# Final RMSNorm of a decoder step on one core: the mean by wide F32 products, the root on ScalarE, the last block in token halves

## The chip, the core and the metric

The kernel runs on one core of one Trainium2 chip. The core has TensorE (PE, matrix products into PSUM), VectorE (DVE), ScalarE (ACT), GpSimd (POOL) and SyncE (SP, which here only issues DMAs). The metric is the time of one execution in microseconds on the device; lower is better. Three runs of the kernel before lasted 1084.12, 1084.95 and 1085.59 us, so the median is 1084.95 us.

## The reference

One layer of a decoder trunk on 256 prompt tokens and 8 x 4 sample tokens with 2048 channels, all in F32, and a final norm over the channels. What matters here is the end:

```python
def rmsnorm(x, g):
    xf = x.astype(jnp.float32)
    y = xf * lax.rsqrt(jnp.mean(xf * xf, axis=-1, keepdims=True) + EPS)
    return (y * g.astype(jnp.float32)).astype(x.dtype)
...
    h2 = rmsnorm(x, norm2_g)
    f = jnp.square(jax.nn.relu(jnp.einsum("btd,df->btf", h2, w_ff1)))
    x = x + jnp.einsum("btf,fd->btd", f, w_ff2)
...
    y_prompt = rmsnorm(xp, norm_f)
    y_sample = rmsnorm(xs, norm_f)
```

Before that stand an input projection, a depthwise convolution with a layernorm, a pooling group and an output projection.

## The kernel before

Activations lie with channels on the partitions: `xT` is 128 x 16 x 288, sixteen blocks k of 128 channels by T = 288 tokens. All weights stream once from HBM in pieces of 128 x 1024 F32. ScalarE rounds each piece to F32R (`whi`, L274), VectorE or GpSimd forms the rest (`wlo`, L279, L282), and `gemm` makes three products for each 128 x 128 weight tile (L305), each with 288 moving columns. The feed-forward part runs in four chunks of 2048 hidden channels: eight groups of the first product, then eight groups g of the second, each group two output blocks k = 2g and 2g + 1.

The order of the instructions on each engine is set by a scheduler that plays the program through; `tc.issue_after(...)` ties a piece of code to stand behind a given instruction.

The second norm (`second_rows`, L638 to L651) comes once, inside the first chunk: a mean by two products with the constant tile `means`, a `Sqrt` on ScalarE (L648), and `inverse_root` (L231 to L236): a reciprocal and one Newton step in three SCALAR_TENSOR_TENSOR operations on VectorE, all 128 x 288 wide.

In the last chunk (`last`, L682 to L692) each block of `xT` gets its product added (L683), ScalarE squares it (L686, L689), VectorE adds the square into `ssf` (L691), and ScalarE multiplies the block by the gain of the final norm (L692). For the last block, k = 15, the square stays in `qf`.

The end of the kernel, from L698:

- L703: the sums over the channels. For each of three runs of 96 tokens, the 96 columns of `ssf`, then of `qf`, are the stationary side and one column of the constant `mean_d` is the moving side. The means stand as 96 x 3 in PSUM (`ends`).
- L706: products `idle<-ones`, three behind the `ssf` sums and four behind the `qf` sums, whose result is not used.
- L708 and `inverse_root`: square root, reciprocal and Newton step on 96 x 3.
- L712: the row spread. Products with the identity put the inverse root of each token on all 128 partitions, once in PSUM as `rows_f` (in `ends`) and once more as `again`.
- `finish` (L716 to L721): VectorE multiplies the blocks 0 to 11 by `rows_f`, read from PSUM, in pieces of 1, 1, 2, 2, 3 and 3 blocks. L724: ScalarE copies `again` to `rf` in SBUF, and GpSimd, which here reads SBUF alone, multiplies the blocks 12 to 15 by `rf`, one by one. Each piece is stored as soon as it is done; the pieces of each engine go in turn to the queue of SP and the queue of ScalarE. One block of the output is 128 x 288 F32, 144 KB; all sixteen are 2304 KB.

Of the kernel before, what the change touches and what calls it, by code (L numbers as in the profile page):

```python
# [9 lines left out]
F32 = mybir.dt.float32  # L10
F32R = mybir.dt.float32r
AF = mybir.ActivationFunctionType
ALU = mybir.AluOpType
# [3 lines left out]
P = 128  # L17
# [3 lines left out]
T = SEQ + NB * NS  # L21
TB = T // 3
# [6 lines left out]
EPS = 1e-6  # L29
KT = D // P  # L30
# [7 lines left out]
ZO = PH + SEQ  # L38
ZL = ZO + NB * ZS
LATER = 1000000  # L40

# [43 lines left out]
def trunk_kernel(ctx: ExitStack, tc: tile.TileContext, io):  # L87
# [3 lines left out]
    nc = tc.nc  # L91

    const = ctx.enter_context(tc.tile_pool(name="const", bufs=1))
# [7 lines left out]
    cvp = ctx.enter_context(tc.tile_pool(name="cvp", bufs=2, space=PSUM))  # L101
# [4 lines left out]
    def nm(s):  # L106
        seen[s] = seen.get(s, 0) + 1
        return f"{s}{seen[s]}"

    @contextmanager  # L110
    def later(by=LATER):

        tc.cur_priority += by
        yield
        tc.cur_priority -= by

    def row(name):
        return rowp.tile([P, T], F32, name=nm(name), tag="row")
# [9 lines left out]
    def tmp(name, n=T, tag="tmp", bufs=2):  # L128
        return tmpp.tile([P, n], F32, name=nm(name), tag=tag, bufs=bufs)

    def ms(name):
        return msp.tile([P, 2, 512], F32, name=nm(name), tag="ms")

    def f32(t):
        return t.bitcast(F32)

    def both(r):

        return r[:, None, :T].to_broadcast([P, 2, T])
# [11 lines left out]
    xT = const.tile([P, KT, T], F32, name="xT")  # L151
# [4 lines left out]
    def v(key, j):  # L156
        return vec[:, OFF[key] + j : OFF[key] + j + 1]
# [45 lines left out]
    ones = const.tile([P, P], F32, name="ones")  # L203
# [3 lines left out]
    def load_table(func, src):  # L207

        return nc.scalar.activation(few[: src.shape[0], :], src, func)
# [5 lines left out]
    ident = const.tile([TB, TB], F32, name="ident", padded_shape=[TB, TB + 40])  # L215
# [7 lines left out]

    means = const.tile([P, P], F32R, name="means")
    nc.vector.tensor_scalar(means, ones, DC / D, None, op0=ALU.mult)
    cst = const.tile([P, 32], F32, name="cst")
    eps, mean_d = cst[:, 0:1], cst[:, 1:2]
    nc.vector.memset(eps, EPS)
    nc.vector.memset(mean_d, 1.0 / D)

    def inverse_root(mean, root, y, out):  # L231

        nc.vector.reciprocal(y, root)
        nc.vector.scalar_tensor_tensor(out=root, in0=mean, scalar=EPS, in1=y, op0=ALU.add, op1=ALU.mult)
        nc.vector.scalar_tensor_tensor(out=root, in0=root, scalar=-0.5, in1=y, op0=ALU.mult, op1=ALU.mult)
        nc.vector.scalar_tensor_tensor(out=out, in0=root, scalar=1.5, in1=y, op0=ALU.add, op1=ALU.mult)  # L236

    def rsqrt_sums(parts, scale, after=None):

# [62 lines left out]
    def mm(*args, **kw):  # L302

        with tc.issue_after(chain[-1]) if chain else nullcontext():
            last = nc.tensor.matmul(*args, **kw)  # L305
        if chain:
            chain[0] = last.ins
        return last
# [37 lines left out]
    def bank2():  # L346
        return acc.tile([P, 2, 512], F32, name=nm("ac"), tag="ac")

    def each(bk):
        return [bk[:, m, :] for m in range(2)]  # L350

    def halves(x2):

        return [(x2[0][:, m, :], x2[1][:, m, :]) for m in range(2)]
# [193 lines left out]
    load_table(AF.Sqrt, f32(mixp[1][0])[:, 0:1])  # L548
    with later(2 * LATER):
        nc.sync.dma_start(io["u_out"], u_all[:, :, UO - CH : UL])  # L550
# [30 lines left out]
    for g in range(8):  # L581
        bk = bank2()
        with behind:
            last = gemm(each(bk), [mixp[k] for k in korder], between=BETWEEN.get(g, {}), classes=TURN if g == 2 else "")
# [5 lines left out]
    for j, c in enumerate(cs):  # L590
        n = tmpp.tile([P, 2, T], F32, name=nm("n"), tag="ag", bufs=2)
# [12 lines left out]
    last = None  # L604
    for g in range(8):
        bk = bank2()
        last = gemm(each(bk), mixc, classes=TURN if g == 2 else "")
# [14 lines left out]
        for m, (ah, al) in enumerate(a2):  # L622
            k = 2 * g + m
            xk = xT[:, k, :]
# [13 lines left out]
    def second_rows():  # L638

        hl = actp.tile([P, 4, T], F32R, name="hl", tag="act")  # L640
        hi, lo = hl[:, 1, :], hl[:, 0, :]
        nc.scalar.copy(hi, ss2)
        nc.vector.tensor_tensor(lo, ss2, f32(hi), op=ALU.subtract)
        bk, r2 = ms("mean2"), row("r2")
        mean, root = bk[:, 0, :T], bk[:, 1, :T]
        mm(mean, means, hi, start=True, stop=False)
        last = mm(mean, means, lo, start=False, stop=True)
        nc.scalar.activation(root, mean, AF.Sqrt, bias=eps)  # L648
        inverse_root(mean, root, r2, r2)
        rows2.append(r2)  # L650
        return last  # L651

    for ch in range(DFF // FCH):
        fx, done = [], []
        for g in range(FCH // 256):
            bk = bank2()
            gemm(each(bk), x1, between={2: second_rows} if ch == 0 and g == 1 else {}, classes="01" * 6 + TURN if ch == 0 and g == 1 else "")
            if ch == 0 and g == 2:
                chain.clear()
            done.append(bk)  # L660
            if ch or g:
                for bk in done:
                    t = tmpp.tile([P, 2, T], F32, name=nm("t"), tag="ag", bufs=2)
                    nc.vector.scalar_tensor_tensor(out=t, in0=bk[:, :, :T], scalar=0.0, in1=both(rows2[0]), op0=ALU.max, op1=ALU.mult)  # L664
                    f = tmpp.tile([P, 2, T], F32, name=nm("f"), tag="ag2", bufs=2)
                    nc.scalar.activation(f, t, AF.Square)
                    fh, fl = act2("fx")
                    nc.scalar.copy(fh, f)
                    nc.vector.tensor_tensor(fl, f, f32(fh), op=ALU.subtract)
                    fx += halves((fh, fl))  # L670
                done = []
        last = ch == DFF // FCH - 1
        for g in range(8):
            bk = bank2()
            banks = each(bk)
            if last and g == 7:
                banks[1] = bank2()[:, 1, :]
            gemm(banks, fx, m_outer=last and g == 7)
            for m in range(2):
                k = 2 * g + m  # L680
                xk = xT[:, k, :]
                if last:  # L682
                    nc.vector.tensor_tensor(xk, xk, banks[m][:, :T], op=ALU.add)  # L683
                    if k == 0:
                        ssf = row("ssf")
                        nc.scalar.activation(ssf, xk, AF.Square)  # L686
                    else:
                        qf = tmp("q")
                        nc.scalar.activation(qf, xk, AF.Square)  # L689
                        if k < KT - 1:  # L690
                            nc.vector.tensor_tensor(ssf, ssf, qf, op=ALU.add)  # L691
                    nc.scalar.activation(xk, xk, AF.Copy, scale=v("norm_f", k))  # L692
                elif m:
                    x2 = xT[:, 2 * g : 2 * g + 2, :]
                    nc.vector.tensor_tensor(x2, x2, bk[:, :, :T], op=ALU.add)  # L695


    ends, again = ms("ends"), cvp.tile([P, 512], F32, name="again", tag="cv")[:, :T]  # L698
    sums_f, rows_f = ends[:TB, 0, 0:3], ends[:, 1, :T]
    idle = cvp.tile([P, 512], F32, name="idle", tag="cv")  # L700
    for n, (part, busy) in enumerate(((ssf, 3), (qf, 4))):
        for j in range(3):
            last = nc.tensor.matmul(sums_f[:, j : j + 1], part[:, j * TB : (j + 1) * TB], mean_d[:, 0:1], start=n + j == 0, stop=n == 1 and j == 2)  # L703
        with tc.issue_after(last.ins):
            for j in range(busy):
                nc.tensor.matmul(idle[:, 0:P], ones, ones, start=True, stop=True)  # L706
    root, first, s_f = [cst[:TB, 2 + 3 * j : 5 + 3 * j] for j in range(3)]
    nc.scalar.activation(root, sums_f, AF.Sqrt, bias=eps[:TB, :])  # L708
    inverse_root(sums_f, root, first, s_f)
    for spread_f in (rows_f, again):  # L710
        for j in range(3):
            nc.tensor.matmul(spread_f[:, j * TB : (j + 1) * TB], s_f[:, j : j + 1].to_broadcast([TB, P]), ident, start=j == 0, stop=j == 2)  # L712
    rf = row("rf")
    queues = (nc.sync, nc.scalar)

    def finish(eng, r, pieces):  # L716

        for j, (k0, n) in enumerate(pieces):
            xk = xT[:, k0 : k0 + n, :]
            eng.tensor_tensor(xk, xk, r[:, None, :].to_broadcast([P, n, T]), op=ALU.mult)  # L720
            queues[j % 2].dma_start(io["yT"][:, k0 : k0 + n, :], xk)  # L721

    finish(nc.vector, rows_f, ((0, 1), (1, 1), (2, 2), (4, 2), (6, 3), (9, 3)))
    nc.scalar.copy(rf, again)  # L724
    finish(nc.gpsimd, rf, [(k, 1) for k in range(12, KT)])


# [56 lines left out]
```

## Time and profile before

| what | value |
|---|---|
| median of three runs | 1084.95 us (1084.12 to 1085.59) |
| profiled execution, span from its first to its last instruction | 1082.8 us |
| mean granted TensorE clock over the span | 0.997 |
| busy: PE, DVE, ACT, POOL | 1071.5, 635.4, 479.0, 173.6 us |
| HBM read, written | 185.16 MB, 4.28 MB |
| TensorE's last product of the last `gemm` ends | 1069.54 us |
| last VectorE and GpSimd multiplication ends | 1077.5 and 1077.6 us |

The page has no time of the profiled execution but its span, which is 2.15 us below the median of the runs. "Span" counts from the first to the last instruction on any engine, the closing waits of SP among them. A row of the timeline has the start, the length, the engine, the line, the operation, what it writes and reads, the shape, and how often it stands there in a row; where it says x6, the length runs from the start of the first to the end of the last. A row of the groups has the busy time of all and the mean of one in ns. Idle time is shown with what ended it.

### The profile page before, as it was taken

How to read it: one execution, taken by the hardware profiler on the slowest of the kernel's cores; microseconds unless marked ns; L12 is line 12 of the kernel's file. 1: busy time of each engine (PE TensorE's matmuls, PEld its weight loads, DVE VectorE, ACT ScalarE, POOL GpSimd, SP SyncE). 2: the span in 40 equal slices, each digit the busy share in tenths (PEclk: the TensorE clock that was granted, in tenths of full speed). 3: DMA queues.
4: the chain of work that ended last, by engine and by line, in shares of the span. 5: the costliest groups of instructions: out<-in, count | busy, mean ns of one | idle time of the engine just before them, and what ended most of it. 6: DMA issues, size and time to landing. Idle time of an engine off the chain costs nothing.

```text
span 1082.8 us, 19572 instructions
## 1 busy us (share of the span) xinstructions
PE 1071.5 (99%) x8198; PEld 1069.9 (99%) x8198; DVE 635.4 (59%) x818; ACT 479.0 (44%) x585; POOL 173.6 (16%) x180
## 2 busy tenths in 40 slices
PE   9999999999999999999999999999999999999996
PEld 9999999999999999999999999999999999999996
DVE  8899999678655544445544444545544445554553
ACT  8654445475544433334443333444433334444441
POOL 0878979512000000000000000000000000000001
PEclk9999999999999999999999999999999999999998
DMA  9896468545555555555555555555555555555522
GB/s 325 281 273 185 137 196 239 176 152 177 173 164 170 172 166 169 174 164 169 171 168 168 175 165 169 174 167 167 174 165 168 174 169 165 173 166 168 173 78 88
DMA packets 58296, 190.71 MB, mean 176 GB/s; under 512 B 6240, under 2 KB 11232, under 8 KB 58208
## 3 DMA queue, kind: packets, MB, share of 16 engines
q1 hardware_dynamic: 56336, 184.35, 53.9%
q0 software_dynamic: 1008, 3.67, 1.9%
q8 instruction: 64, 1.05, 0.4%
q10 hardware_dynamic: 864, 1.44, 0.4%
q14 instruction: 24, 0.20, 0.1%
HBM read 185.16 MB, written 4.28 MB: 175 GB/s over the span
## 4 chain that ended last, share of the span: by engine, by line
PE 77%; issue 20%; ACT 1%; DVE 0%; DMA 0%; POOL 0%; POOLq 0%
PE ac L305 77%; PE pp L305 1%; DMA wr<-in_w 0%; ACT whi L274 0%; POOL xT L720 0%; ACT n L595 0%; DVE wlo L279 0%; PE pt L305 0%; PE pmean L305 0%; POOLq L770 0%; DVE xT L695 0%; DVE n L592 0%; ACT whi L364 0%; ACT mx L597 0%; DVE hx L367 0%
## 5 line engine op out<-in xcount | busy, mean ns | idle before, releaser
L274 ACT CAST whi<-wr 128x1024 fp32r<-128x1024 f32 (+1 forms) x332 | 348.0, 1049 | 551.4 <-PE ac L305 533.5
L279 DVE TENSOR_TENSOR wlo<-wr,whi 128x1024 fp32r<-128x1024 f32 x288 | 353.1, 1226 | 348.5 <-ACT whi L274 348.5
L305 PE MATMUL ac<-ax,whi 128*128 128x288 f32 x2048 | 351.0, 292 | 0.0
L305 PE MATMUL ac<-fx,whi 128*128 128x288 f32 x2048 | 350.2, 292 | 0.0
L305 PEld LDWEIGHTS ac<-ax,whi 128*128 128x128 f32 x2048 | 296.0, 187 | 0.0
L305 PEld LDWEIGHTS ac<-fx,whi 128*128 128x128 f32 x2048 | 295.6, 187 | 0.0
L305 PE MATMUL ac<-ax,wlo 128*128 128x288 f32 x1024 | 217.4, 292 | 0.0
L305 PE MATMUL ac<-fx,wlo 128*128 128x288 f32 x1024 | 216.4, 292 | 0.0
L305 PEld LDWEIGHTS ac<-ax,wlo 128*128 128x128 f32 x1024 | 162.6, 187 | 0.0
L305 PEld LDWEIGHTS ac<-fx,wlo 128*128 128x128 f32 x1024 | 162.3, 187 | 0.0
L305 PE MATMUL ac<-hx,whi 128*128 128x288 f32 x768 | 131.8, 295 | 1.2 <-DVE hx L367 1.2
L720 POOL TENSOR_TENSOR xT<-xT,rf 128x288 f32<-128x288 f32 x4 | 3.1, 795 | 800.1 <-ACT rf L724 800.1
L305 PEld LDWEIGHTS ac<-hx,whi 128*128 128x128 f32 x768 | 112.1, 190 | 1.4 <-ACT hx L369 1.4
L282 POOL TENSOR_TENSOR wlo<-wr,whi 128x512 fp32r<-128x512 f32 x74 | 100.3, 1410 | 35.3 <-ACT whi L274 34.3
L461 DVE SCALAR_TENSOR_TENSOR pc<-u_all,vec,pc 128x256 f32<-128x256 f32 x232 | 99.5, 483 | 1.9 <-ACT pc L458 0.7
L305 PE MATMUL ac<-hx,wlo 128*128 128x288 f32 x384 | 80.1, 294 | 0.0
L305 PEld LDWEIGHTS ac<-hx,wlo 128*128 128x128 f32 x384 | 61.1, 190 | 0.0
L305 PE MATMUL ac<-dx,whi 128*128 128x288 f32 x256 | 46.0, 296 | 0.0
L305 PE MATMUL ac<-mx,whi 128*128 128x288 f32 x256 | 45.1, 294 | 0.1
L664 DVE SCALAR_TENSOR_TENSOR t<-ac,r 128x576 f32<-128x576 f32 x32 | 24.2, 758 | 25.1 <-PE ac L305 25.1
L305 PEld LDWEIGHTS ac<-dx,whi 128*128 128x128 f32 x256 | 38.0, 188 | 0.2
L305 PEld LDWEIGHTS ac<-mx,whi 128*128 128x128 f32 x256 | 37.5, 188 | 0.6 <-ACT mx L597 0.4
(133 smaller groups left out, 533.6 us busy)
## 6 DMA issues: line engine op xcount, KB each, us to landing
wr<-in_w SPq DMA_DIRECT2D x335, 512.0 KB, 3.8
wlo<-in_w POOLq DMA_DIRECT2D x7, 512.0 KB, 7.7
xT<-in_xT SPq DMA_DIRECT2D x8, 288.0 KB, 7.3
wr<-in_w SPq DMA_DIRECT2D x5, 256.0 KB, 3.6
out_u_out<-u_all SPq DMA_DIRECT2D x1, 1208.0 KB, 9.3
u_all<-in_hist_c SPq DMA_DIRECT2D x8, 136.0 KB, 6.2
out_z_out<-z_all SPq DMA_DIRECT2D x1, 668.0 KB, 9.9
z_all<-in_hist_p SPq DMA_DIRECT2D x4, 152.0 KB, 7.5
```

Of the source, the lines that this page charges most:

```text
L274: nc.scalar.copy(hi, raw)
L279: nc.vector.tensor_tensor(lo, raw, f32(hi), op=ALU.subtract)
L282: nc.gpsimd.tensor_tensor(lo[:, j : j + 2, :], raw[:, j : j + 2, :], f32(hi[:, j : j + 2, :]), op=ALU.subtract)
L305: last = nc.tensor.matmul(*args, **kw)
L461: nc.vector.scalar_tensor_tensor(out=dst, in0=up[:, w : w + SEQ], scalar=cwv[:, w : w + 1], in1=pc, op0=ALU.mult, op1=ALU.add)
L664: nc.vector.scalar_tensor_tensor(out=t, in0=bk[:, :, :T], scalar=0.0, in1=both(rows2[0]), op0=ALU.max, op1=ALU.mult)
L720: eng.tensor_tensor(xk, xk, r[:, None, :].to_broadcast([P, n, T]), op=ALU.mult)
```

## The change

Five things, all in the norms:

- `mean_d` becomes a constant tile of 128 x 128. The mean of the final norm is made by products in which `mean_d` is the stationary side and 144 token columns of `ssf` or `qf` the moving side, so that each mean stands on all 128 partitions at once. The products of L703, the unused products of L706 and the row spread of L712 go, and the copy of L724 with them.
- `inverse_root` takes ScalarE's `Abs_reciprocal_sqrt` for the first value in place of `Sqrt` and VectorE's reciprocal; three SCALAR_TENSOR_TENSOR operations stay. Both norms use it. In the final norm it now works on 128 x 144 twice, from PSUM into `rf` in SBUF.
- The last block, k = 15, is added and squared in two token halves, and the root is made for each half. Its gain is multiplied in behind the second root.
- VectorE and GpSimd both multiply by `rf` in SBUF.
- VectorE's pieces are now 1, 1, 1, 1, 2, 3 and 3 blocks.

```diff
+HALVES = (slice(0, T // 2), slice(T // 2, T))
...
-    cst = const.tile([P, 32], F32, name="cst")
-    eps, mean_d = cst[:, 0:1], cst[:, 1:2]
+    eps = const.tile([P, 32], F32, name="cst")[:, 0:1]
     nc.vector.memset(eps, EPS)
+    mean_d = const.tile([P, P], F32, name="mean_d")
     nc.vector.memset(mean_d, 1.0 / D)
-    def inverse_root(mean, root, y, out):
-        nc.vector.reciprocal(y, root)
-        nc.vector.scalar_tensor_tensor(out=root, in0=mean, scalar=EPS, in1=y, op0=ALU.add, op1=ALU.mult)
-        nc.vector.scalar_tensor_tensor(out=root, in0=root, scalar=-0.5, in1=y, op0=ALU.mult, op1=ALU.mult)
-        nc.vector.scalar_tensor_tensor(out=out, in0=root, scalar=1.5, in1=y, op0=ALU.add, op1=ALU.mult)
+    def inverse_root(mean, half, y):
+        root = nc.scalar.activation(y, mean, AF.Abs_reciprocal_sqrt, bias=eps)
+        nc.vector.scalar_tensor_tensor(out=half, in0=y, scalar=-0.5, in1=y, op0=ALU.mult, op1=ALU.mult)
+        nc.vector.scalar_tensor_tensor(out=half, in0=mean, scalar=EPS, in1=half, op0=ALU.add, op1=ALU.mult)
+        nc.vector.scalar_tensor_tensor(out=y, in0=half, scalar=1.5, in1=y, op0=ALU.add, op1=ALU.mult)
+        return root
...
-        nc.scalar.activation(root, mean, AF.Sqrt, bias=eps)
-        inverse_root(mean, root, r2, r2)
+        inverse_root(mean, tmp("q"), r2)
...
+                if last and k == KT - 1:
+                    qf = tmp("q")
+                    for h in HALVES:
+                        nc.vector.tensor_tensor(xk[:, h], xk[:, h], banks[m][:, h], op=ALU.add)
+                    for h in HALVES:
+                        nc.scalar.activation(qf[:, h], xk[:, h], AF.Square)
...
+    ends, rf, step = ms("ends"), row("rf"), tmp("q")
+    for n, h in enumerate(HALVES):
+        total = ends[:, n, h]
+        for part in (ssf, qf):
+            nc.tensor.matmul(total, mean_d, part[:, h], start=part is ssf, stop=part is qf)
+    for n, h in enumerate(HALVES):
+        root = inverse_root(ends[:, n, h], step[:, h], rf[:, h])
+    with tc.issue_after(root.ins):
+        nc.scalar.activation(xT[:, KT - 1, :], xT[:, KT - 1, :], AF.Copy, scale=v("norm_f", KT - 1))
...
-            eng.tensor_tensor(xk, xk, r[:, None, :].to_broadcast([P, n, T]), op=ALU.mult)
+            eng.tensor_tensor(xk, xk, rf[:, None, :].to_broadcast([P, n, T]), op=ALU.mult)
...
-    finish(nc.vector, rows_f, ((0, 1), (1, 1), (2, 2), (4, 2), (6, 3), (9, 3)))
-    nc.scalar.copy(rf, again)
-    finish(nc.gpsimd, rf, [(k, 1) for k in range(12, KT)])
+    finish(nc.vector, ((0, 1), (1, 1), (2, 1), (3, 1), (4, 2), (6, 3), (9, 3)))
+    finish(nc.gpsimd, [(k, 1) for k in range(12, KT)])
```

The scheduler leaves the order of all engines as it was up to the second norm and again from there to the last block, but for a few neighbours behind the second norm that change places. The end is another program. VectorE before, from the last block on (in brackets the engines that an instruction waits for):

```order
L683 TENSOR_TENSOR xT<-xT,ac_11386 128x288 [waits PE_49]
L233 RECIPROCAL cst<-cst 96x3 [waits Activation_49]
L234 SCALAR_TENSOR_TENSOR cst<-ends_11492,cst 96x3 [waits DVE_49,PE_49]
L235 SCALAR_TENSOR_TENSOR cst<-cst 96x3 [waits DVE_49]
L236 SCALAR_TENSOR_TENSOR cst<-cst 96x3 [waits DVE_49]
L720 TENSOR_TENSOR xT<-xT,ends_11492 128x288 [waits PE_49]
L720 TENSOR_TENSOR xT<-xT,ends_11492 128x288
L720 TENSOR_TENSOR xT<-xT,ends_11492 128x576 x2
L720 TENSOR_TENSOR xT<-xT,ends_11492 128x864 x2
```

VectorE now, at the same place (`q_11496` is `step`; the line numbers are the new ones):

```order
L686 TENSOR_TENSOR xT<-xT,ac_11387 128x144 [waits PE_49]
L686 TENSOR_TENSOR xT<-xT,ac_11387 128x144
L235 SCALAR_TENSOR_TENSOR q_11496<-rf_11495 128x144 [waits DVE_49,Activation_49]
L236 SCALAR_TENSOR_TENSOR q_11496<-ends_11494,q_11496 128x144 [waits DVE_49,PE_49]
L237 SCALAR_TENSOR_TENSOR rf_11495<-q_11496,rf_11495 128x144 [waits DVE_49]
L235 SCALAR_TENSOR_TENSOR q_11496<-rf_11495 128x144 [waits Activation_49]
L236 SCALAR_TENSOR_TENSOR q_11496<-ends_11494,q_11496 128x144 [waits DVE_49]
L237 SCALAR_TENSOR_TENSOR rf_11495<-q_11496,rf_11495 128x144 [waits DVE_49]
L719 TENSOR_TENSOR xT<-xT,rf_11495 128x288 [waits DVE_49]
L719 TENSOR_TENSOR xT<-xT,rf_11495 128x288 x3
L719 TENSOR_TENSOR xT<-xT,rf_11495 128x576
L719 TENSOR_TENSOR xT<-xT,rf_11495 128x864 x2
```

Six operations on 128 x 144 stand where four on 96 x 3 stood, and the multiplications read `rf` where they read `ends`. ScalarE with its queue before, from the last block's square on:

```order
L689 ACTIVATE q_11489<-xT 128x288 [waits DVE_49]
L692 ACTIVATE xT<-xT,vec 128x288 [waits Activation_49]
L708 ACTIVATE cst<-ends_11492,cst 96x3 [waits PE_49]
L724 COPY rf_11519<-again 128x288 [waits PE_49]
L721 DMA out_yT<-xT 128x288 [waits DVE_49]
L721 DMA out_yT<-xT 128x576 [waits DVE_49]
L721 DMA out_yT<-xT 128x288 [waits Pool_49]
L721 DMA out_yT<-xT 128x864 [waits DMAHW5_49,DVE_49]
L721 DMA out_yT<-xT 128x288 [waits DMAHW6_49,Activation_49,Pool_49]
```

And now:

```order
L688 ACTIVATE q_11489<-xT 128x144 [waits DVE_49] x2
L234 ACTIVATE rf_11495<-ends_11494,cst 128x144 [waits PE_49]
L234 ACTIVATE rf_11495<-ends_11494,cst 128x144 [waits DVE_49]
L712 ACTIVATE xT<-xT,vec 128x288 [waits Activation_49]
L720 DMA out_yT<-xT 128x288 [waits DVE_49]
L720 DMA out_yT<-xT 128x288 [waits Pool_49]
L720 DMA out_yT<-xT 128x288 [waits DVE_49]
L720 DMA out_yT<-xT 128x864 [waits DVE_49]
L720 DMA out_yT<-xT 128x288 [waits DMAHW6_49,Pool_49]
```

The gain of block 15 moved behind the second root, and the second root waits for VectorE: in the built program for its L236 of the first half, which reads the same PSUM tile. The first root waits for the last of the four products, so for both halves. In ScalarE's queue the stores are those of the blocks 1, 13, 3, 6 to 8 and 15, in this order; in SP's queue those of 0, 12, 2, 4 to 5, 14 and 9 to 11.

More of the change, by code (lines that the diff above doesn't have):

```diff
@@ L644, in second_rows @@
         bk, r2 = ms("mean2"), row("r2")
-        mean, root = bk[:, 0, :T], bk[:, 1, :T]
+        mean = bk[:, 0, :T]
         mm(mean, means, hi, start=True, stop=False)
         last = mm(mean, means, lo, start=False, stop=True)
-        nc.scalar.activation(root, mean, AF.Sqrt, bias=eps)
-        inverse_root(mean, root, r2, r2)
+        inverse_root(mean, tmp("q"), r2)
         rows2.append(r2)
@@ L681, in trunk_kernel @@
                 xk = xT[:, k, :]
-                if last:
+                if last and k == KT - 1:
[4 more added lines that the diff above has]
+                        nc.scalar.activation(qf[:, h], xk[:, h], AF.Square)
+                elif last:
                     nc.vector.tensor_tensor(xk, xk, banks[m][:, :T], op=ALU.add)
@@ L689, in trunk_kernel @@
                         nc.scalar.activation(qf, xk, AF.Square)
-                        if k < KT - 1:
-                            nc.vector.tensor_tensor(ssf, ssf, qf, op=ALU.add)
+                        nc.vector.tensor_tensor(ssf, ssf, qf, op=ALU.add)
                     nc.scalar.activation(xk, xk, AF.Copy, scale=v("norm_f", k))
@@ L695, in trunk_kernel, with finish @@
                     nc.vector.tensor_tensor(x2, x2, bk[:, :, :T], op=ALU.add)
[L698 to L713, printed above, removed]
+    ends, rf, step = ms("ends"), row("rf"), tmp("q")
[7 more added lines that the diff above has]
+        nc.scalar.activation(xT[:, KT - 1, :], xT[:, KT - 1, :], AF.Copy, scale=v("norm_f", KT - 1))
     queues = (nc.sync, nc.scalar)
-    def finish(eng, r, pieces):
+    def finish(eng, pieces):
         for j, (k0, n) in enumerate(pieces):
             xk = xT[:, k0 : k0 + n, :]
-            eng.tensor_tensor(xk, xk, r[:, None, :].to_broadcast([P, n, T]), op=ALU.mult)
+            eng.tensor_tensor(xk, xk, rf[:, None, :].to_broadcast([P, n, T]), op=ALU.mult)
             queues[j % 2].dma_start(io["yT"][:, k0 : k0 + n, :], xk)
-    finish(nc.vector, rows_f, ((0, 1), (1, 1), (2, 2), (4, 2), (6, 3), (9, 3)))
-    nc.scalar.copy(rf, again)
-    finish(nc.gpsimd, rf, [(k, 1) for k in range(12, KT)])
+    finish(nc.vector, ((0, 1), (1, 1), (2, 1), (3, 1), (4, 2), (6, 3), (9, 3)))
+    finish(nc.gpsimd, [(k, 1) for k in range(12, KT)])
 def kernel(**inputs):
```

## The prediction

> **What bounds the kernel now.** I read the page first, then the chain of waits.
>
> ```profile
> span 1082.8 us, 19572 instructions
> PE 1071.5 (99%) x8198; PEld 1069.9 (99%) x8198; DVE 635.4 (59%) x818; ACT 479.0 (44%) x585; POOL 173.6 (16%) x180
> ```
> ```profile
> 0.72 3.89 DMA wr<-in_w
> ...
> 284.77 572.63 PE ac L305 x4404
> ```
>
> TensorE is busy 99% of the span, and the chain shows its products back to back for 572 us from the second norm on. Up to the last product only TensorE counts. So the second norm's edit gets nothing: its reciprocal and root are hidden behind products, and the order keeps its table load where it was. The larger `mean_d` memset, one operation on a VectorE that waits for the first weights (0.72 to 4.61), is hidden too. Without that cover it would cost what a 128 x 128 memset takes more than a 128 x 1 one, a tenth of a us. What is left is the tail. This is the timeline from the last product on:
>
> ```profile
> 1069.12 0.42 PE L305 MATMUL ac<-fx,whi 128*128 128x288 f32 x2
> ...
> 1069.58 0.46 DVE L683 TENSOR_TENSOR xT<-xT,ac 128x288 f32<-128x288 f32 x1 [4.81 <-PE ac L305]
> ...
> 1070.07 0.45 ACT L689 ACTIVATE q<-xT 128x288 f32<-128x288 f32 x1 [5.22 <-DVE xT L683]
> ...
> 1070.59 0.65 PE L703 MATMUL ends<-cst,q 128*96 128x1 f32 x6
> ...
> 1071.10 1.14 PE L706 MATMUL idle<-ones 128*128 128x128 f32 x8
> 1071.27 0.26 ACT L708 ACTIVATE cst<-ends,cst 96x3 f32<-96x3 f32 x1 [0.19 <-PE ends L703]
> 1071.57 0.17 DVE L233 RECIPROCAL cst<-cst 96x3 f32<-96x3 f32 x1 [1.53 <-ACT cst L708]
> 1071.85 0.16 DVE L234 SCALAR_TENSOR_TENSOR cst<-ends,cst 96x3 f32<-96x3 f32 x1
> 1072.04 0.16 DVE L235 SCALAR_TENSOR_TENSOR cst<-cst 96x3 f32<-96x3 f32 x1
> ...
> 1072.45 0.91 PE L712 MATMUL ends<-ident,cst 96*128 96x96 f32 x6 [0.21 <-DVE cst L236]
> ...
> 1073.39 4.08 DVE L720 TENSOR_TENSOR xT<-xT,ends 128x288 f32<-128x288 f32 x6 [1.00 <-PE ends L712]
> 1073.88 3.54 SPq L721 DMA_DIRECT2D out_yT<-xT  x5
> ...
> 1074.54 3.05 POOL L720 TENSOR_TENSOR xT<-xT,rf 128x288 f32<-128x288 f32 x4 [800.07 <-ACT rf L724]
> ```
>
> The last product ends at 1069.54; add, square, sums, root, spread; at 1073.39 VectorE begins to multiply, at 1073.88 the first store is issued. The multiplications end at 1077.5, the span 5.3 us later. The DMA rows of 1068 to 1083, in slices of 0.375 us, say why:
>
> ```profile
> GB/s 0 0 0 0 0 0 0 0 0 0 0 0 0 0 0 0 0 15 350 378 178 399 363 418 399 390 449 387 415 357 449 427 396 323 200 22 0 0 0 0
> ```
>
> Bytes move from about 1074.73 (the 15 fills the end of its slice), 0.85 us after the first issue, to about 1081.15, at a mean of 404 GB/s between the dip (178) and the decline. Sixteen blocks of 147,456 bytes need 5.84 us at that rate. Stores are the limit of the tail, with one small hole; 1.65 us of landing and closing waits follow them. A later first store, or a hole, moves the end.
>
> **The change, part by part.** These groups carry the durations:
>
> ```profile
> L626 DVE SCALAR_TENSOR_TENSOR ax<-xT,vec,ax 128x288 fp32r<-128x288 f32 x16 | 15.9, 1033 | 0.0
> L643 DVE TENSOR_TENSOR hl<-ss,hl 128x288 fp32r<-128x288 f32 x1 | 0.5, 450 | 0.0
> L235 DVE SCALAR_TENSOR_TENSOR mean<-mean,r 128x288 f32<-128x288 f32 x1 | 0.5, 460 | 0.0
> L720 DVE TENSOR_TENSOR xT<-xT,ends 128x288 f32<-128x288 f32 x2 | 0.8, 452 | 1.0 <-PE ends L712 1.0
> L720 DVE TENSOR_TENSOR xT<-xT,ends 128x576 f32<-128x576 f32 x2 | 1.4, 749 | 0.0
> L720 DVE TENSOR_TENSOR xT<-xT,ends 128x864 f32<-128x864 f32 x2 | 2.0, 1050 | 0.0
> L648 ACT ACTIVATE mean<-mean,cst 128x288 f32<-128x288 f32 x1 | 0.5, 477 | 0.0
> ```
>
> *Add and square in halves.* VectorE takes 0.30 us per 288 columns and 0.15 fixed, so 0.30 for 144. Two halves end at 1070.10, the whole at 1070.04. The second half square (0.32, cut the same way) then ends near 1070.50, as the whole does now (1070.52). Nothing won; the first half square ends at 1070.24.
>
> *Sums.* An F32 product stands as two rows of TensorE. Now six short rows bring the root to 1071.27. Then, from 1070.31: two rows for the first half of `qf`, two of `ssf`, two for the second half of `qf`, 144 columns each. The unused 128-column products step by 0.12 (eight in 1.14, less a last one of 0.29); a long row of the stream steps by 0.13 for 288 columns. At least 0.12, at most 0.26 a row if F32 streamed every column twice at that pace; I take 0.13, nearest the 128-column row. The products end at 1071.22, the first root begins at 1071.25. Nothing again. The filler products that go lay beside waits.
>
> *Root.* Between 0.26 (3 columns) and 0.48 (288) stands 0.37 for 144. By the Trainium skill ("ScalarE: Activation LUTs", section "What ACT_TABLE_LOAD costs") an ACTIVATE with a pointer bias takes 280 ns and 0.833 ns a column, an estimate of 0.40; the sum below would be 0.06 us higher. Each half has three VectorE operations of 0.31 (between 0.16 for 3 columns and 0.46 for 288), with the gaps of the rows above: 0.03, and 0.10 ahead of the first that reads PSUM. The halves do not run beside each other: the second root waits for L236 of the first half. So: root 1071.62; L235 1071.96; L236 1072.37; second root 1072.77; L235 1073.11; L236 1073.46; L237 1073.81. Gone are the 96 x 3 steps, the spread and its 0.94 us, and the copy to `rf`. Behind the second root ScalarE holds the gain of block 15 (done before 1073.5, due for GpSimd's last block) and stores that come later still, so its wait delays VectorE alone. VectorE's first multiplication begins at 1073.84, 0.45 later than now; GpSimd's at 1073.89, 0.65 earlier.
>
> *The multiplications.* This is the large term. Now VectorE reads `ends` in PSUM and `xT` in SBUF, GpSimd two SBUF tiles, and both run at once: 4.08 and 3.05 us side by side. Then VectorE reads two SBUF tiles as well. Around 254 us such a pair stands in the trace:
>
> ```profile
> 253.76 1.99 POOL L633 TENSOR_TENSOR ss<-ss,q 128x288 f32<-128x288 f32 x2 [4.25 <-ACT q L632]
> ```
> ```profile
> 252.88 1.23 DVE L279 TENSOR_TENSOR wlo<-wr,whi 128x1024 fp32r<-128x1024 f32 x1 [0.33 <-ACT whi L274]
> 254.02 2.05 DVE L626 SCALAR_TENSOR_TENSOR ax<-xT,vec,ax 128x288 fp32r<-128x288 f32 x2
> ```
>
> Two VectorE operations of 128 x 288 that take 0.46 alone end 2.05 us after the first's start, two of GpSimd in 1.99: the L626 group has a mean of 1033 ns against 450 for L643. From L279's end (254.11) to the last one's (256.07) two of each take 1.96: 0.98 a pair, one after the other, of which GpSimd's part is 0.67 (the last VectorE operation ends 0.32 after the last of GpSimd). The Trainium skill ("SBUF — State Buffer", section "SBUF: two separate sides") says it as a rule: VectorE with two SBUF inputs and GpSimd share a port pair that one holds for a whole instruction. The trace agrees.
>
> So: block 0 until 1074.29; then GpSimd and VectorE in turn, three pairs and one more of GpSimd (3.61) until 1077.90; the two-block piece, whose waiting part is done, 0.62, until 1078.52; the three-block pieces 0.97 each (1.05 less the 0.08 that neighbours overlap: six means add up to 4.50, the row says 4.08), until 1079.49 and 1080.46.
>
> *The stores.* The first six blocks leave one by one. Each moves in 0.37 us and two come every 0.98, so the DMA runs dry between them: the smaller pieces close the old hole, the slower engines open larger ones. Ten blocks (4 to 5, 14, 6 to 8, 15, 9 to 11) remain from 1078.55 on, since the stores of 14 and 15 stand in their queues behind the larger pieces. They begin to move at 1079.40, need 3.65 us at 404 GB/s, end at 1083.05 in place of 1081.15: 1.9 us later. The last piece, issued at 1080.49, is there before its turn.
>
> *Sum.* Span 1082.8 + 1.9 = 1084.7. The runs' median stands 2.15 over the span shown, by what lies around it and is untouched: 1084.95 + 1.9 = 1086.9 us, 0.18% more. The runs spread over 1.5 us; about 0.2%, 2.2 us, is what a measurement can tell from no change. So the forecast is a loss just under that bound.
>
> **The rivals.**
>
> *No taking of turns* (chance 0.14). If VectorE's multiplications do not contend here, they end 4.1 us after 1073.84 at 1078.0, GpSimd's near 1077.0; stores begin 0.45 later, without the hole, and move until 1081.0: 1084.8 us. For it speaks that the three-block pieces alone could keep the DMA busy; against it L626 at 1033 ns.
>
> *Slow F32 products* (0.18). With the 144-column rows at 0.26 the root begins 0.8 later, and all behind it: 1087.7, slower by more than 0.2%. It passes that bound from 0.17 a row (0.24 us over six rows on top of 0.13). No F32 row of such a width with a full stationary side stands in the trace; the 128-column row speaks against it, for it only that its step may be set by its weight load, which a wider row need not share.
>
> *The clock* (0.03). The filler products may have held it up.
>
> ```profile
> 1070.00:1075.00 5.00, 3.81 (x32) 3.45 (x31) 2.29 (x9) 1.65 (x4) 0.46 (x1) 1.00 0.05 18
> 1075.00:1078.00 3.00, 0.00 (x0) 0.00 (x0) 2.47 (x3) 0.00 (x0) 2.59 (x4) 0.59 0.99 367
> ```
>
> At half clock the six rows cost 0.8 more, 1087.7 again. But the grant was still 1.00 in the window in which the products end (1074.02), and the changed kernel idles TensorE only some 0.4 us before its last products.
>
> *Halves that do overlap* are no case of their own: were the first root ready at 1070.8, half a us would go off the forecast.
>
> **How the numbers follow.** The forecast has 0.65: 0.49 within 0.2%, 0.16 above, since roots and gaps on a chain of ten steps can be wrong by half a us (1086.2 to 1087.6 is its own range). Slower: 0.16 + 0.18 + 0.03 = 0.37. Same: 0.49 + 0.13 of the first rival = 0.62. Faster: 0.01. The range takes in the first rival with 0.2 for the measurement, 1084.6, and at the top the slow products with as much, 1087.9; under 1 in 10 lies outside.
>
> **What would show it.** Right: VectorE's first multiplication near 1073.8 (counted from a last product at 1069.54); GpSimd's four at about 1.0 us each in place of 0.8, VectorE's blocks 1 to 3 at about 1.0 in place of 0.45; the last VectorE piece ending near 1080.5; GB/s with gaps ahead of 1079 and a solid stretch behind. Wrong: both engines' means as now (first rival); the sums' rows stepping by over 0.17 us (second); a clock below 1.00 there (third); or any change of TensorE's time ahead of 1069.5.

## The result and the profile after

| | median, us | range of the runs | ratio to the kernel before (95% interval) |
|---|---|---|---|
| before | 1084.88 | 1083.54 to 1086.17 (21 runs) | |
| after | 1086.46 | 1085.31 to 1087.47 (21 runs) | 1.0014 (1.0008 to 1.0019) |

The changed kernel is slower by 1.58 us, 0.14%; the interval, times 1084.88, is 0.9 to 2.1 us. The profiled execution has a span of 1084.7 us against 1082.8 before. The first lines of its page show that TensorE still bounds everything ahead of the tail:

```profile
span 1084.7 us, 19519 instructions
PE 1067.6 (98%) x8168; PEld 1065.4 (98%) x8168; DVE 637.5 (59%) x821; ACT 477.4 (44%) x586; POOL 174.6 (16%) x180
```

The timeline from the last product on (start and duration in us; in brackets the idle time ahead and what ended it) has the whole change in it:

```profile
1068.96 0.42 PE L307 MATMUL ac<-fx,whi 128*128 128x288 f32 x2
...
1069.42 0.52 DVE L686 TENSOR_TENSOR xT<-xT,ac 128x144 f32<-128x144 f32 x2 [4.82 <-PE ac L307]
1069.76 0.54 ACT L688 ACTIVATE q<-xT 128x144 f32<-128x144 f32 x2 [5.08 <-DVE xT L686]
...
1070.14 0.51 PE L708 MATMUL ends<-q,mean_d 128*128 128x144 f32 x2 [0.51 <-ACT q L688]
...
1070.49 0.41 PE L708 MATMUL ends<-ssf,mean_d 128*128 128x144 f32 x2
...
1070.73 0.41 PE L708 MATMUL ends<-q,mean_d 128*128 128x144 f32 x2
1071.18 0.38 ACT L234 ACTIVATE rf<-ends,cst 128x144 f32<-128x144 f32 x1 [0.88 <-PE ends L708]
1071.59 0.31 DVE L235 SCALAR_TENSOR_TENSOR q<-rf 128x144 f32<-128x144 f32 x1 [1.65 <-ACT rf L234]
1072.00 0.31 DVE L236 SCALAR_TENSOR_TENSOR q<-ends,q 128x144 f32<-128x144 f32 x1
1072.35 0.31 DVE L237 SCALAR_TENSOR_TENSOR rf<-q,rf 128x144 f32<-128x144 f32 x1
1072.35 0.38 ACT L234 ACTIVATE rf<-ends,cst 128x144 f32<-128x144 f32 x1 [0.79 <-DVE q L236]
...
1073.79 6.55 DVE L719 TENSOR_TENSOR xT<-xT,rf 128x288 f32<-128x288 f32 x7
1073.90 3.89 POOL L719 TENSOR_TENSOR xT<-xT,rf 128x288 f32<-128x288 f32 x4 [799.59 <-DVE rf L237]
1074.27 6.42 SPq L720 DMA_DIRECT2D out_yT<-xT  x6
```

Two rows carry the reading. The second root (1072.35) is released by L236 of the first half, so the halves go one behind the other. And the multiplications take VectorE 6.55 us where they took 4.08. The groups of both engines in the tail (busy us, mean ns) say why; the first row is GpSimd's of before:

```profile
L720 POOL TENSOR_TENSOR xT<-xT,rf 128x288 f32<-128x288 f32 x4 | 3.1, 795 | 800.1 <-ACT rf L724 800.1
```
```profile
L719 POOL TENSOR_TENSOR xT<-xT,rf 128x288 f32<-128x288 f32 x4 | 3.9, 1001 | 799.6 <-DVE rf L237 799.6
L719 DVE TENSOR_TENSOR xT<-xT,rf 128x288 f32<-128x288 f32 x4 | 3.3, 896 | 0.0
L719 DVE TENSOR_TENSOR xT<-xT,rf 128x864 f32<-128x864 f32 x2 | 2.0, 1046 | 0.0
L719 DVE TENSOR_TENSOR xT<-xT,rf 128x576 f32<-128x576 f32 x1 | 1.3, 1341 | 0.0
```

One block costs VectorE 896 ns in place of 452 (the first, begun ahead of GpSimd, 457; the three behind it 1041 to 1046), the two-block piece 1341 in place of 749; the three-block pieces, which run when GpSimd is done (1077.79), cost what they did (1046). The single operations in the trace end in turn: VectorE at 1074.24, GpSimd at 1074.89, VectorE at 1075.21, GpSimd at 1075.86, and so on to GpSimd's last at 1077.79; VectorE about 0.32 us behind GpSimd each time, GpSimd 0.65 behind VectorE. The bytes of the stores in slices of 0.375 us from 1068 to 1083:

```profile
GB/s 0 0 0 0 0 0 0 0 0 0 0 0 0 0 0 0 0 0 3 347 123 372 332 224 384 181 89 301 3 0 375 409 372 449 433 363 412 439 396 277
```

There are holes up to 1079.25 and a solid stretch of ten blocks behind it, which ends at 1083.17.

**How executions are compared.** TensorE's last products do not lie at the same time in each execution: the first half add begins at 1069.42 here, the add of before at 1069.58, and in the experiments between 1068.33 and 1070.49. The difference is there before the weights' long stream begins. Two rows of this kernel and the same two of the last experiment, whose stream ends 1.09 us earlier, show it (first the first product of `ac` from `dx`, then the last two products of the stream):

```profile
164.54 0.43 PE L307 MATMUL ac<-dx,whi 128*128 128x288 f32 x2
...
1068.96 0.42 PE L307 MATMUL ac<-fx,whi 128*128 128x288 f32 x2
```
```profile
163.47 0.43 PE L307 MATMUL ac<-dx,whi 128*128 128x288 f32 x2
...
1067.87 0.42 PE L307 MATMUL ac<-fx,whi 128*128 128x288 f32 x2
```

From row to row it is 904.42 and 904.40 us, and in all ten traces 904.39 to 904.43. One thing that differs ahead of these rows is the granted clock, which becomes full at 4.59 us here and at 10.57 before, at 10.34 in e7, which begins as this kernel does, and at 5.80 in e3, which begins as before. The edit may have a part in it: in the seven traces of kernels that begin as this one (after, e1, e2, e5 to e8) the add begins at 1068.33 to 1069.50, in the three others (before, e3, e4) at 1069.58 to 1070.49. No run settles whether that is chance. So I count from the start of the last block's first add: up to VectorE's first multiplication (the chain), and from there to the end of the span (the finish). Before: 3.81 and 9.41, together 13.2. After: 4.37 and 10.91, together 15.3. The tail is 2.1 us longer, 0.56 of it chain, 1.50 finish. The spans differ by 1.9 because this stream ended 0.16 earlier. The runs' 1.58 us is less than the tail's 2.1, which lies at the upper end of their interval; a gain of some tenths of a us ahead of the tail would do that, and so would noise.

### The profile page after: what moved, and what is told of

It is laid out like the page before. It is cut to its first block, busy times and chain, and to the rows that moved or that the text cites. A ratio compares the mean times of both kernels' runs of the same rounds, so it can differ in the third digit from the quotient of the medians.

```text
span 1084.7 us, 19519 instructions
## 1 busy us (share of the span) xinstructions
PE 1067.6 (98%) x8168; PEld 1065.4 (98%) x8168; DVE 637.5 (59%) x821; ACT 477.4 (44%) x586; POOL 174.6 (16%) x180
## 3 DMA queue, kind: packets, MB, share of 16 engines
q10 hardware_dynamic: 864, 1.29, 0.3%
## 4 chain that ended last, share of the span: by engine, by line
PE 96%; DMA 1%; DVE 1%; ACT 1%; issue 0%; DVEq 0%
PE ac L307 95%; DMA wlo<-in_w 1%; PE pp L307 1%; DVE xT L719 1%; DMA wr<-in_w 0%; ACT whi L276 0%; ACT n L597 0%; DVE wlo L281 0%; PE pt L307 0%; PE ends L708 0%; PE pmean L307 0%; DVEq L768 0%; ACT rf L234 0%; DVE n L594 0%; DVE q L235 0%
## 5 line engine op out<-in xcount | busy, mean ns | idle before, releaser
L719 POOL TENSOR_TENSOR xT<-xT,rf 128x288 f32<-128x288 f32 x4 | 3.9, 1001 | 799.6 <-DVE rf L237 799.6
```

What stands on the lines that cost most here:

```text
L719: eng.tensor_tensor(xk, xk, rf[:, None, :].to_broadcast([P, n, T]), op=ALU.mult)
```

## The experiments

Each was timed against the kernel before on the same chip (median 1084.63 us in the first four, 1084.52 in the others).

| kernel | chain, us | finish, us | of it to 14 blocks, us | median, us | ratio to before (interval) |
|---|---|---|---|---|---|
| before | 3.81 | 9.4 | 6.82 | 1084.88 | |
| after | 4.37 | 10.9 | 8.45 | 1086.46 | 1.0014 (1.0008 to 1.0019) |
| e1, VectorE's rows in PSUM | 4.80 | 9.7 | 6.69 | 1085.37 | 1.0007 (0.9998 to 1.0016) |
| e2, VectorE alone | 4.36 | 9.6 | 7.10 | 1085.30 | 1.0006 (0.9997 to 1.0015) |
| e3, before with its rows in SBUF | 4.24 | 10.8 | 7.90 | 1086.69 | 1.0021 (1.0012 to 1.0029) |
| e4, before with the small pieces | 3.81 | 9.7 | 6.70 | 1085.08 | 1.0004 (0.9995 to 1.0012) |
| e5, halves apart | 3.16 | 10.9 | 8.45 | 1085.15 | 1.0005 (0.9996 to 1.0014) |
| e6, halves apart, VectorE alone | 3.15 | 9.5 | 6.93 | 1083.90 | 0.9994 (0.9986 to 1.0003) |
| e7, a queue for each engine | 4.36 | 10.3 | 7.94 | 1086.01 | 1.0012 (1.0003 to 1.0021) |
| e8, e6 without the Newton step | 1.95 | 9.5 | 6.92 | 1082.06 | 0.9977 (0.9969 to 0.9986) |

The third figure counts, within the finish, up to the moment at which the DMA packets of the trace had moved the bytes of fourteen of the sixteen blocks. Behind it lie the last two blocks and the closing waits. These two blocks took 0.93 to 0.96 us in seven of the traces, but 1.29 in e1, 1.37 in e3 and 1.42 in e4. In just these three an 8 KB packet of the instruction queue, 0.31 us long, lies among the last stores; in the others it starts as the last store ends. So the finish of e1, e3 and e4 holds some 0.4 us that their edits need not have caused.

Theory: the finish is longer because VectorE and GpSimd, both with two SBUF inputs, take turns, and the chain because the halves wait for each other. Rivals: the smaller pieces, and the order of the stores in their queues.

**e1: VectorE's rows in PSUM, the rest as after.** One copy puts the finished rows into a PSUM tile for VectorE; GpSimd reads the SBUF ones.

```diff
+    rows_f = cvp.tile([P, 512], F32, name="rows_f", tag="cv")[:, :T]
+    nc.scalar.copy(rows_f, rf)
...
-    finish(nc.vector, ((0, 1), (1, 1), (2, 1), (3, 1), (4, 2), (6, 3), (9, 3)))
-    finish(nc.gpsimd, [(k, 1) for k in range(12, KT)])
+    finish(nc.vector, rows_f, ((0, 1), (1, 1), (2, 1), (3, 1), (4, 2), (6, 3), (9, 3)))
+    finish(nc.gpsimd, rf, [(k, 1) for k in range(12, KT)])
```

> The changed kernel, but ScalarE copies rf into PSUM and VectorE multiplies by that copy, as it did before the change; GpSimd goes on reading rf in SBUF. Taking turns: VectorE has one SBUF input again, so its means go back to 0.45, 0.75 and 1.05 us and GpSimd's to 0.80; VectorE starts 0.45 us later for the copy and yet ends near 1078.7 instead of 1080.3; the span falls by 1.4 to 1.8 us to about 1083.1, and the time stands within 0.4 us of the kernel before. Late start (the rival: the loss comes from the first store being 0.4 us later and from the store order, not from the two engines): the copy makes VectorE later still, the span grows by 0.3 to 0.5 us to about 1085.1.

The same groups, in its tail:

```profile
L721 POOL TENSOR_TENSOR xT<-xT,rf 128x288 f32<-128x288 f32 x4 | 3.0, 794 | 799.6 <-DVE rf L237 799.6
L721 DVE TENSOR_TENSOR xT<-xT,rows_f 128x864 f32<-128x864 f32 x2 | 2.0, 1044 | 0.0
L721 DVE TENSOR_TENSOR xT<-xT,rows_f 128x288 f32<-128x288 f32 x4 | 1.5, 447 | 0.5 <-ACT rows_f L712 0.5
L721 DVE TENSOR_TENSOR xT<-xT,rows_f 128x576 f32<-128x576 f32 x1 | 0.7, 745 | 0.0
```

With one operand of VectorE in another memory, and a copy ahead of it, 896 ns is 447 again, GpSimd's 1001 is 794, and the finish falls by 1.2 us, by 1.8 up to the fourteenth block, to what it was before. VectorE's part of this would look the same if two SBUF inputs made it slow by themselves; e2 rules that out. The time came out 0.74 us above before and not told apart from it, and the interval overlaps with that of after, so it is the trace that shows this. The copy lengthens the chain by 0.43, which is why only 0.8 of the 1.2 comes out of the tail, less than the 1.4 to 1.8 expected of the span.

**e2: VectorE does GpSimd's four blocks as well.**

```diff
-    finish(nc.gpsimd, [(k, 1) for k in range(12, KT)])
+    finish(nc.vector, [(k, 1) for k in range(12, KT)])
```

> The changed kernel, but blocks 12 to 15 are multiplied by VectorE too, one by one behind its other pieces, and GpSimd does nothing. Taking turns: without GpSimd nothing holds VectorE up; its eleven pieces need about 5.5 us, end near 1079.3, a us before VectorE's seven do in the changed kernel, and the DMA runs without holes; the span falls by 1.5 to 2.0 us to 1082.7 to 1083.2. Late start, where VectorE is slow for a reason of its own: four more blocks of 0.4 to 1.0 us each come behind 1080.3, the span grows by 1 to 4 us.

VectorE's rows in its timeline, and the group of its single blocks:

```profile
1068.74 0.52 DVE L686 TENSOR_TENSOR xT<-xT,ac 128x144 f32<-128x144 f32 x2 [4.82 <-PE ac L307]
...
1073.10 5.64 DVE L719 TENSOR_TENSOR xT<-xT,rf 128x288 f32<-128x288 f32 x11
```
```profile
L719 DVE TENSOR_TENSOR xT<-xT,rf 128x288 f32<-128x288 f32 x8 | 3.1, 451 | 0.0
```

One engine with two SBUF inputs does all sixteen blocks in 5.64 us, less than the 6.55 that it needs for twelve beside GpSimd. A single block takes 451 ns, so two SBUF inputs do not slow VectorE while GpSimd is still. With e1 this leaves the taking of turns. The finish is 1.3 us shorter than after (1.5 to 2.0 was expected of the span), and GpSimd's help is worth less than nothing here.

**e3: the kernel before, its rows in SBUF for both engines.** The second spread is left out and ScalarE copies the first one to `rf`, which both engines read.

```diff
-    for spread_f in (rows_f, again):
+    for spread_f in (rows_f,):
...
-    finish(nc.vector, rows_f, ((0, 1), (1, 1), (2, 2), (4, 2), (6, 3), (9, 3)))
-    nc.scalar.copy(rf, again)
+    nc.scalar.copy(rf, rows_f)
+    finish(nc.vector, rf, ((0, 1), (1, 1), (2, 2), (4, 2), (6, 3), (9, 3)))
```

> The kernel before, with one thing of the change: both engines multiply by rf in SBUF, which ScalarE copies from the first spread (the second spread goes). VectorE starts near 1073.85, as in the changed kernel; sums, root, Newton step, spread and piece sizes are those of before. Taking turns: single blocks at about 1.0 us on both engines, two-block pieces at about 1.35; the span grows by 1.3 to 1.9 us over before, nearly the whole loss. Late start: 0.45 us later, everything else as before, the span grows by 0.3 to 0.5 us.

Its groups:

```profile
L720 POOL TENSOR_TENSOR xT<-xT,rf 128x288 f32<-128x288 f32 x4 | 4.6, 1166 | 799.4 <-ACT rf L723 799.4
L720 DVE TENSOR_TENSOR xT<-xT,rf 128x864 f32<-128x864 f32 x2 | 2.6, 1343 | 0.0
L720 DVE TENSOR_TENSOR xT<-xT,rf 128x576 f32<-128x576 f32 x2 | 2.6, 1342 | 0.0
L720 DVE TENSOR_TENSOR xT<-xT,rf 128x288 f32<-128x288 f32 x2 | 1.4, 753 | 1.4 <-ACT rf L723 1.4
```

The loss appears in a kernel that has nothing else of the change: the finish grows by 1.4 us, by 1.1 up to the fourteenth block, and the copy adds 0.43 to the chain. VectorE's twelve blocks take 6.48 us where they took 4.08. GpSimd waits too, and the longer for VectorE's longer pieces: 1166 ns a block beside pieces of two and three blocks, 1001 beside single ones.

**e4: the kernel before with the smaller pieces.**

```diff
-    finish(nc.vector, rows_f, ((0, 1), (1, 1), (2, 2), (4, 2), (6, 3), (9, 3)))
+    finish(nc.vector, rows_f, ((0, 1), (1, 1), (2, 1), (3, 1), (4, 2), (6, 3), (9, 3)))
```

> The kernel before, with VectorE's pieces of 1, 1, 1, 1, 2, 3 and 3 blocks. Both theories: the dip in the store stream near 1075.6 closes, and with the stores as the limit the span falls by 0.1 to 0.3 us; nothing else moves.

The bytes of 1068 to 1083:

```profile
GB/s 0 0 0 0 0 0 0 0 0 0 0 0 0 0 0 0 0 0 138 363 387 384 381 360 390 396 415 439 396 344 446 387 409 399 259 12 9 0 0 0
```

The dip to 178 is gone, and the fourteenth block is through 0.12 us sooner (6.70 for 6.82), as the expected gain of 0.1 to 0.3 would have it, though the slices hold only 360 to 390 GB/s while the single blocks move and mostly 390 to 446 behind them. The finish is nevertheless 9.7 in place of 9.4: the last bytes trickle (259, 12, 9) around the packet of the instruction queue (1080.78 to 1081.09). The timed runs cannot tell this kernel from before.

**e5: the halves apart.** After, with each half's mean in a PSUM tile of its own, the products of `ssf` ahead of those of `qf`, both roots one behind the other, and the six VectorE steps alternating between the halves.

```diff
+    ends = [cvp.tile([P, 512], F32, name=nm("ends"), tag="cv")[:, h] for h in HALVES]
+    for part in (ssf, qf):
+        for total, h in zip(ends, HALVES):
...
+    for total, h in zip(ends, HALVES):
+        root = nc.scalar.activation(rf[:, h], total, AF.Abs_reciprocal_sqrt, bias=eps)
+    for h in HALVES:
...
```

> The changed kernel, its halves made independent: the two ssf products come first, the means of the halves lie in two PSUM tiles, both roots follow at once and VectorE's six operations alternate between the halves. Multiplications and stores stay. Counted from the start of the last block's first add, VectorE's first multiplication stood at 4.37 us in the changed kernel and at 3.81 before. If the waits between the halves cost what the forecast has for them, it comes at 3.2 to 3.4; GpSimd and VectorE still take turns (means near 1.0), so everything behind it moves by the same 1.0 us and no more: the time falls by 0.8 to 1.1 us against the changed kernel, to a ratio near 1.0005 to before. Rival: the tail is set by the stores' own pace and hides the chain; then the time falls by less than 0.3 us.

Its timeline:

```profile
1068.63 0.52 DVE L686 TENSOR_TENSOR xT<-xT,ac 128x144 f32<-128x144 f32 x2 [4.81 <-PE ac L307]
...
1069.90 0.65 ACT L710 ACTIVATE rf<-ends,cst 128x144 f32<-128x144 f32 x2 [0.39 <-PE ends L708]
...
1071.79 6.55 DVE L725 TENSOR_TENSOR xT<-xT,rf 128x288 f32<-128x288 f32 x7
```

The first root begins 1.27 us after the add (1.76 in after), since the products of `ssf` no longer stand between those of `qf` and it waits for the first half's product alone: the four rows of `qf` end at 1070.11, behind its start. The second needs no L236. What each of these is worth was not taken apart. The chain falls from 4.37 to 3.16. The multiplications still take 6.55 us and the finish 10.9: the chain was shortened without touching the finish.

**e6: e5, and VectorE alone.** GpSimd's blocks go to VectorE, in pieces of growing size.

```diff
-    finish(nc.vector, ((0, 1), (1, 1), (2, 1), (3, 1), (4, 2), (6, 3), (9, 3)))
-    finish(nc.gpsimd, [(k, 1) for k in range(12, KT)])
+    finish(nc.vector, ((0, 1), (1, 1), (2, 1), (3, 1), (4, 2), (6, 2), (8, 2), (10, 3), (13, 3)))
```

> As the run with independent halves, and VectorE multiplies all sixteen blocks in pieces of 1, 1, 1, 1, 2, 2, 2, 3 and 3; GpSimd does nothing. Taking turns: no contention, first multiplication 3.2 to 3.4 us behind the last add, a store stream without holes of about 7.5 us from the first issue; the time falls by 1.8 to 2.3 us against the changed kernel and stands 0.1 to 0.5 us below the kernel before. Rival (VectorE alone is too slow for sixteen blocks): it ends above the kernel before by 0.5 us or more.

Its timeline, from the same add:

```profile
1069.07 0.52 DVE L686 TENSOR_TENSOR xT<-xT,ac 128x144 f32<-128x144 f32 x2 [4.82 <-PE ac L307]
...
1072.22 5.50 DVE L725 TENSOR_TENSOR xT<-xT,rf 128x288 f32<-128x288 f32 x9
```

Both terms are gone, and the tail is 12.6 us, 0.6 less than before and 2.7 less than after. It beats after (the intervals 0.9986 to 1.0003 and 1.0008 to 1.0019 do not meet); against before its 0.06% stays within the uncertainty.

**e7: a store queue for each engine.** SP's queue takes VectorE's pieces, ScalarE's takes GpSimd's.

```diff
-    finish(nc.vector, ((0, 1), (1, 1), (2, 1), (3, 1), (4, 2), (6, 3), (9, 3)))
-    finish(nc.gpsimd, [(k, 1) for k in range(12, KT)])
+    finish(nc.vector, nc.sync, ((0, 1), (1, 1), (2, 1), (3, 1), (4, 2), (6, 3), (9, 3)))
+    finish(nc.gpsimd, nc.scalar, [(k, 1) for k in range(12, KT)])
```

> The changed kernel, but all of VectorE's stores go to SP's queue and all of GpSimd's to ScalarE's, so that the stores of the blocks 14 and 15 no longer stand behind VectorE's larger pieces. If that standing behind is a part of the loss, these two leave while the DMA is idle (near 1077.7 and 1078.7), eight blocks in place of ten remain from 1079.3 on, and the end comes 0.6 to 0.8 us earlier. Rival: VectorE's last pieces alone set the end; then it moves by less than 0.2 us. Turns, chain and GpSimd's means stay as in the changed kernel.

VectorE's row and that of ScalarE's queue:

```profile
1073.86 6.55 DVE L717 TENSOR_TENSOR xT<-xT,rf 128x288 f32<-128x288 f32 x7
...
1075.00 3.23 ACTq L718 DMA_DIRECT2D out_yT<-xT  x4
```

The four stores of GpSimd are issued by 1078.23, as its blocks come, and no longer behind VectorE's larger pieces. The profiled finish is 0.57 us shorter than after, just below the 0.6 to 0.8 expected; the medians, 1.49 and 1.58 above before, do not tell the two kernels apart. So the order of the stores costs at most part of the loss: VectorE's 6.55 is unchanged. And it costs that only once the turns have delayed the pieces, for e1 sends the same pieces to the same queues as after and is through its fourteenth block no later than before.

**e8: e6 without the Newton step.** The three VectorE operations per half that refine the root are left out in the final norm, which prices them.

```diff
-    for h in HALVES:
-        nc.vector.scalar_tensor_tensor(out=step[:, h], in0=rf[:, h], scalar=-0.5, in1=rf[:, h], op0=ALU.mult, op1=ALU.mult)
...
```

> As the run with independent halves and VectorE alone, but the Newton step of the final norm is left out: the value of ScalarE's root is used as it is. The chain loses VectorE's six operations: first multiplication near 2.0 us behind the last add, 1.2 earlier than with them; since nothing else is late the whole tail follows, and the time falls by 1.0 to 1.3 us against that run, to a ratio of about 0.9985 to before. Rival (stores' own pace hides the chain): less than 0.4 us.

The first multiplication in its timeline:

```profile
1068.33 0.52 DVE L686 TENSOR_TENSOR xT<-xT,ac 128x144 f32<-128x144 f32 x2 [4.82 <-PE ac L307]
...
1070.28 5.51 DVE L719 TENSOR_TENSOR xT<-xT,rf 128x288 f32<-128x288 f32 x9 [1.43 <-ACT rf L710]
```

The chain falls by 1.2 us to 1.95, the finish stays, and the time is 0.23% under before. In the tail, what is taken from the chain comes off the end one for one. The median fell by 1.84 us against e6, more than the 1.0 to 1.3 expected; the profiled stream ended 0.74 earlier here, and the two intervals (0.9986 to 1.0003 and 0.9969 to 0.9986) leave room for either figure.

## Why the prediction came out as it did

The forecast was a loss of 1.9 us, just under 0.2%, out of two terms: VectorE's later start and the turns behind it. The runs say 1.58 (0.9 to 2.1), the tail 2.1. The mechanism was the one forecast, and the runs show each of its terms; two sizes were off. That the profiled span hit the forecast 1084.7 is in part luck, as the tail came out 0.16 us longer than forecast and the stream ended 0.16 earlier. That about 0.2% was the least a measurement could tell was too cautious: over 21 runs each, 0.14% stands clear of no change. Step by step:

- **The second norm and the memset win and cost nothing: as forecast.** The stream of products takes 904.4 us from `dx` to its end in this kernel as in the others. That the memset costs nothing in the start-up was only argued: the drift there, some 2 us between executions, is larger than the 0.1 us forecast for it, and the kernels that have it begin their stream no later than the others.
- **Add and square in halves: as forecast.** The adds end 0.52 us after their start (0.52 forecast), the squares 0.88 (0.92).
- **The sums, 0.13 a row: the step of the chain that was too small.** The four later rows step by 0.12, so the second rival, slow F32 products, is out. But the pair of rows behind the wait has 0.51 us where the others have 0.41: the first row after the wait steps by about 0.23. Set on the same last product, the first root comes 0.09 late, and this 0.1 runs on to the first multiplication.
- **Root and Newton steps: as forecast, within 0.02 each.** 0.38 for a root of 0.37, 0.31 for a step of 0.31. For the root the Trainium skill ("ScalarE: Activation LUTs", section "What ACT_TABLE_LOAD costs") led to an estimate of 0.40; the measured 381 ns lie between, nearer the value interpolated from the rows. That the second root waits for L236 of the first half stands in the trace as a release, and e5 shows its price along with that of the first root's wait for both halves and of the order of the products: 1.2 us.
- **First multiplication: 0.56 later than before, 0.45 forecast.** The 0.56 repeats: 4.36 and 4.36 in e2 and e7, 3.81 in e4.
- **The turns: as forecast.** 6.55 us from the first multiplication to VectorE's end against 6.62; 1001 ns of GpSimd's block against 0.98 a pair. The ends alternate at 0.32 and 0.65 us, as the pair at 254 us had it (0.32 and 0.67). e1 and e2 take the turns away and 1.2 to 1.3 us of the finish go; e3 brings them into the kernel before and 1.1 come by the fourteenth block. The first rival, no taking of turns, is out. The section "SBUF: two separate sides" of the Trainium skill's "SBUF — State Buffer", which the prediction drew on, is borne out: VectorE pays with both inputs in SBUF (896 ns), and with one in PSUM it does not (447).
- **"The smaller pieces close the old hole": right.** e4 shows that they close it, and that the fourteenth block is through 0.12 us sooner for it. That e4's finish is longer all the same is its last two blocks, beside the instruction packet.
- **The stores, an end 1.9 later: as forecast, 0.3 short.** Ten blocks stood to the end, as forecast; with the earlier last product taken off (0.16), they were forecast from 1079.24 to 1082.89, and moved from 1079.25 to 1083.17. They began on time, since the turns gave back (6.55 for 6.62) most of what the sums had cost, and needed 3.92 us where 3.65 stood. The rate was right: the nine slices from 1079.25 to 1082.62 hold a mean of 405 GB/s, where 404 was forecast. What the sum left out is the run-out, in which the last bytes move slower: 277 GB/s in the slice up to 1083 and little behind it. The row of before ends so too (323, 200), and the forecast had taken its mean ahead of that decline.
- **The clock: not in play in the tail.** It was 1.00 up to the last product of the sums, as this row of the windows shows (the third column from the right is the granted clock):

```profile
1069.00:1071.20 2.20, 1.63 (x11) 1.20 (x10) 0.52 (x2) 0.56 (x3) 0.00 (x0) 1.00 0.00 0
```

So the finish's 1.5 us goes to the turns: up to the fourteenth block after needs 8.45 us, e1 without them 6.69 and before 6.82, and the smaller pieces alone (e4) cost nothing there. e7's 0.6, the order of the stores, lies inside this part, since it is the turns that push the pieces back. That rests on single profiles; kernels alike in their finish agree there within 0.01 us (after and e5, e1 and e4, e6 and e8). The timed runs alone show the loss of after, the turns together with a copy (e3), and the gain of removing both terms (e6 against after).

## What to carry to other kernels

Before an operand moves from PSUM to SBUF, look who else works at that moment: VectorE beside GpSimd, both with two SBUF inputs, worked in turn (6.55 us where the two, not held up, took 4.1 and 3.1 side by side), and VectorE alone was quicker than the pair (5.5 to 5.6). Cutting a chain in halves brought no overlap while the halves shared a tile and stood one behind the other in the program: the chain was 0.56 us longer than before with one half written out after the other, and 0.65 shorter with the halves apart and interleaved. And where runs drift from the start-up, compare the stage that was edited from its own first event.

## What the runs showed of the hardware beside that

- The stores' packets took 51 ns for 1152 bytes, 93 for 2304 and 135 for 3456 at the median (a piece of one, two and three blocks). Over the 16 DMA engines that works out, as an estimate, at 361, 396 and 410 GB/s, so a piece of one block would move 12% slower than one of three. In e4 the slices of its single blocks held 360 to 390.
- An F32 product of 128 x 144 with a full stationary side steps by 0.12 us a row at full clock, and the first behind a wait by 0.23.
- The granted clock fell to half at 1072.97, 1.8 us after the last product, and 2.6 us earlier than before (1075.53). The full-clock stretches of the kernels lasted 1064.96, 1068.37 or 1071.79 us, 3.41 us apart each. The Trainium skill ("TensorE: Matmul & The Clock Gate", Part 1) tells of a free-running window of 3413 ns, and the trace agrees. It cost nothing here, since no product came behind it.
